# Up projection of a gated MLP: split weights in half units, spread over a column's seven products

## The chip, the cores and the metric

The kernel runs on one core of a Trainium2 chip. The metric is the device time of one execution in microseconds (us); in the profiled execution 1.81 us of it lie outside the span that the profiler records. TensorE is called PE in the rows, VectorE DVE, ScalarE ACT, GpSimd POOL and SyncE, which issues the DMAs, SP.

## The reference, cut to what matters

One encoder block on 16 meta and 1024 tokens with a model width of 1024. Its mixers run first; the change lies in what follows them: the output projection with the second norm, the up projection with a short convolution and a gate, and the first steps of the down projection. D_FF is 2816.

```python
h = h + merged @ w_out

f = dw_conv_centred(rms_norm(h, norm_ffn_w) @ w_ffn_up, w_ffn_conv, b_ffn_conv)
fg, fu = _split(f, (D_FF, D_FF))
return h + (jax.nn.silu(fg) * fu) @ w_ffn_down
```

## The kernel before, in words

Every float32 product is made of three: each operand is split into a high part (a cast on ScalarE) and a low part (the operand less its high part, on VectorE), and TensorE adds hi x hi, hi x lo and lo x hi. For weights that is `wsplit` (cast L1078, low part L1079) in the up stage and `wload` (load L132, L135, L136) elsewhere.

The **out-projection** runs in two rounds of tokens, r = 0 and 1. Each output tile d takes two column blocks, which VectorE evicts from PSUM with the residual added (L1052); ScalarE squares them and GpSimd adds the squares up (L1059). Behind round 0 comes its norm, in three steps (`scale`, `first`, `rest`) that are issued behind tiles d = 1, 2, 3 of round 1: a product with ones, a square root and reciprocals (L1017), eight multiplications on VectorE (L1022), sums on GpSimd (L1026, L1027, L1035) and the splits of seven operands b11, t2, t1, t3, b21, t4, b22 (L1008, L1009). Round 1's norm runs inside the first column of the up stage.

The **up stage** goes over 22 columns j. A column is one product of 2 x 2 blocks in a Strassen-Winograd scheme: seven block products of 12 matmuls each, in the two rounds (256 and 258 token columns), in the order b11, t2, t1, t3, b21, t4, b22, both rounds of a product together from column 1 on. Its weights a11, a12, a21, a22 come in two loads of 512 KB (L1090) into two raw buffers. Four sums on GpSimd (L1098 to L1101) make the combined blocks and are written over the raw ones. The splits of a column are three tiles of 1024 columns (each two blocks) and one of 512, in a ring of five tiles, and stand behind products b11/t2, t3, b21 and t4.

PSUM is evicted with the scheme's additions: ScalarE copies b11 and b21 (L1136, L1156), VectorE adds for t2 (L1141), t3 and t1 (L1151, L1152), t4 (L1160) and b22 (L1164). Then comes the convolution of the column before, over the two halves of f: a middle tap on GpSimd (L1174), two side taps on VectorE (L1175, L1176), Silu on ScalarE (L1178), the gate's product on GpSimd (L1181) and the store of `act` (L1182).

The **down stage** loads act tiles, splits them (L1236, L1237) and its own weights (`wload`), multiplies (PSUM tile psw) and adds (L1258).

Each engine runs its instructions in one fixed order, made when the kernel is built; a waiting instruction holds up what stands behind it. Tiles are reused in rings: a write waits for the last reader of the buffer's tile before.

## Time and profile before

| | |
|---|---|
| median of 3 runs | 2532.42 us (2527.24 to 2540.96) |
| profiled execution | 2529.71 us |
| its span | 2527.9 us |
| granted TensorE clock, mean | 0.977 |
| busy: PE / DVE / ACT / POOL | 94% / 51% / 31% / 34% of the span |
| up stage | about 1762 to 2255 us of the span |

The busy share is a mean over stages with different limits. The granted clock is in parts of full speed: 1.00 is 2.4 GHz, 0.50 is 1.2 GHz, and a value between them means that a stretch held both. An idle time in brackets names what ended it.

### The profile page before, as it was taken

The page shows a single profiled execution, that of the slowest core. Times are in us where ns is not written, and L with a number is a line of the kernel's source. Part 1 is how long each engine was busy: PE and PEld are TensorE (multiplying, and loading weights), DVE is VectorE, ACT ScalarE, POOL GpSimd, SP SyncE. Part 2 cuts the span into 40 slices and gives each one's busy share as a digit, 9 for nine tenths or more (in the row PEclk, how much of TensorE's full clock was granted, in tenths as well). Part 3 has the DMA queues.
Part 4 walks back from the last instruction along what each step waited for, and adds up shares of the span by engine and source line. Part 5 has one row for each costly group of instructions (what it writes and reads, how often), then busy time and mean ns, then how long its engine had stood idle before and what let it go on. Part 6 is the DMA issues. An engine that isn't in the chain of part 4 may idle for free. (4 is left out here: it accounts for less than half of the span.)

```text
span 2527.9 us, 38787 instructions
## 1 busy us (share of the span) xinstructions
PE 2387.7 (94%) x15836; PEld 2230.3 (88%) x15836; DVE 1290.1 (51%) x1822; ACT 771.7 (31%) x1320; POOL 853.9 (34%) x873
## 2 busy tenths in 40 slices
PE   7999999999899899989998999998899999989997
PEld 6999999988798788879887999997799999978887
DVE  6243344545635643663474442436766666665437
ACT  4312211333432532443234221223322222222204
POOL 2121222135514623641461122224355555540003
PEclk9999999999899999999998999999899999999999
DMA  4111112125723751572466552353122122245112
GB/s 146 50 48 41 51 49 61 54 87 158 167 55 126 164 104 63 175 157 45 139 169 168 175 151 90 98 156 113 60 81 76 68 75 76 76 148 194 67 49 68
DMA packets 132499, 259.09 MB, mean 102 GB/s; under 512 B 17441, under 2 KB 75297, under 8 KB 128225
## 3 DMA queue, kind: packets, MB, share of 16 engines
q1 hardware_dynamic: 132320, 256.62, 34.6%
q8 instruction: 124, 2.03, 0.4%
q14 instruction: 55, 0.44, 0.1%
HBM read 199.36 MB, written 57.20 MB: 101 GB/s over the span
## 5 line engine op out<-in xcount | busy, mean ns | idle before, releaser
L143 PE MATMUL psd<-uh,whi 128*128 128x342 f32 (+3 forms) x1376 | 462.5, 336 | 6.8 <-ACT gs L289 6.8
L144 PE MATMUL psd<-ul,whi 128*128 128x342 f32 (+3 forms) x1376 | 443.5, 322 | 0.0
L145 PE MATMUL psd<-uh,wlo 128*128 128x342 f32 (+3 forms) x1376 | 442.6, 322 | 0.0
L136 DVE TENSOR_TENSOR wlo<-wraw,whi 128x1024 fp32r<-128x1024 f32 (+1 forms) x144 | 190.5, 1323 | 217.1 <-ACT whi L135 216.8
L135 ACT CAST whi<-wraw 128x1024 fp32r<-128x1024 f32 (+1 forms) x144 | 149.3, 1039 | 482.7 <-PE psd L144 281.6
L143 PEld LDWEIGHTS psd<-uh,whi 128*128 128x128 f32 (+1 forms) x1376 | 261.1, 190 | 15.7 <-issue 7.2
L144 PEld LDWEIGHTS psd<-ul,whi 128*128 128x128 f32 (+1 forms) x1376 | 260.5, 189 | 7.1 <-issue 6.8
L145 PEld LDWEIGHTS psd<-uh,wlo 128*128 128x128 f32 (+1 forms) x1376 | 260.5, 189 | 0.1
L143 PE MATMUL psd<-whi,uh 128*128 128x256 f32 x768 | 232.6, 303 | 0.6 <-ACT uh L217 0.6
L145 PE MATMUL psd<-whi,ul 128*128 128x256 f32 x768 | 216.0, 281 | 3.3 <-POOL ul L219 2.7
L144 PE MATMUL psd<-wlo,uh 128*128 128x256 f32 x768 | 216.1, 281 | 0.0
L1079 DVE TENSOR_TENSOR wlo<-wraw,whi 128x1024 fp32r<-128x1024 f32 x88 | 112.6, 1284 | 113.7 <-ACT whi L1078 113.6
L143 PEld LDWEIGHTS psd<-whi,uh 128*128 128x128 f32 x768 | 145.3, 189 | 11.9 <-issue 9.1
L143 PE MATMUL psw<-ah,whi 128*128 128x512 f32 (+1 forms) x400 | 148.5, 373 | 5.9 <-ACT ah L1236 5.9
L144 PEld LDWEIGHTS psd<-wlo,uh 128*128 128x128 f32 x768 | 145.7, 190 | 5.8 <-issue 5.3
L144 PE MATMUL psw<-al,whi 128*128 128x512 f32 (+1 forms) x400 | 149.0, 373 | 1.0 <-DVE al L1237 1.0
L145 PEld LDWEIGHTS psd<-whi,ul 128*128 128x128 f32 x768 | 145.1, 189 | 4.1 <-POOL ul L219 3.1
L145 PE MATMUL psw<-ah,wlo 128*128 128x512 f32 (+1 forms) x400 | 146.4, 367 | 0.0
L1078 ACT CAST whi<-wraw 128x1024 fp32r<-128x1024 f32 x88 | 81.5, 940 | 201.4 <-POOL wraw L1101 100.3
L143 PE MATMUL psd<-krh,whi 128*128 128x342 f32 x384 | 123.6, 322 | 3.2 <-ACT krh L932 3.2
L144 PE MATMUL psd<-krl,whi 128*128 128x342 f32 x384 | 123.7, 322 | 0.3 <-DVE krl L933 0.3
L145 PE MATMUL psd<-krh,wlo 128*128 128x342 f32 x384 | 123.4, 322 | 0.0
(304 smaller groups left out, 6123.3 us busy)
## 6 DMA issues: line engine op xcount, KB each, us to landing
br<-row SPq DMA_DIRECT2D x32, 1024.0 KB
wraw<-in_w_up SPq DMA_DIRECT2D x44, 512.0 KB
gt<-gate SPq DMA_DIRECT2D x72, 171.0 KB
wraw<-in_w_xbc SPq DMA_DIRECT2D x24, 512.0 KB
act<-hb SPq DMA_DIRECT2D x22, 512.0 KB
ar<-act SPq DMA_DIRECT2D x22, 512.0 KB
wraw<-in_w_dn SPq DMA_DIRECT2D x19, 512.0 KB
gate<-gs SPq DMA_DIRECT2D x48, 171.0 KB
```

The costliest lines, as they stand in the source:

```text
L135: nc.scalar.copy(hi[:, :n], raw[:, :n])
L136: nc.vector.tensor_sub(lo[:, :n], raw[:, :n], hi[:, :n].bitcast(F32))
L143: nc.tensor.matmul(ps, ah, bh, start=(i == 0), stop=False)
L144: nc.tensor.matmul(ps, ah, bl, start=False, stop=False)
L145: nc.tensor.matmul(ps, al, bh, start=False, stop=(i == n - 1))
L1078: nc.scalar.copy(hi[:, :n], src)
L1079: nc.vector.tensor_sub(lo[:, :n], src, hi[:, :n].bitcast(F32))
```

## The change

Weights are split in units of one block (512 columns): seven casts and seven low parts a column, into a ring of ten half tiles. Each split stands behind one of the seven products: those of column j + 1 called s4 to s7 behind the first four products of column j, s1 to s3 of column j + 2 behind its last three. The loads of column j + 2 are issued at the start of column j, into four raw buffers: two of `wraw` for odd columns, two rows of hb for even ones. The first sum (now L1102) goes to a buffer of its own. The convolution is spread likewise: both middle taps behind the first product, the side taps of one half behind the second, Silu and the other side taps behind the third, the gate's product behind the fifth. The norm is cut into 17 small steps: two token blocks by themselves, multiplications in groups of four on 256 or 258 columns (L1023), issued three at a time. The first four act tiles are loaded ahead into the raw buffers (L1234), and high and low part of act share one tile. In the changed kernel the product is L1132, the load L1095, the sums L1102, L1103, L1104 and L1117, the evictions L1149, L1154, L1164, L1165, L1169, L1173 and L1177, the convolution L1187, L1192, L1193, L1196 and L1199.

```diff
-        def scale():
-            for b0, bn in RB[r]:
-                ps = pm.tile([P, 512], F32, name="psn", tag="psm")
-                a = acc[:, b0 - t0:b0 - t0 + bn]
-                nc.tensor.matmul(ps[:, :bn], ones, a, start=True, stop=True)
-                nc.scalar.activation(a, ps[:, :bn], AF.Sqrt, bias=eps, scale=1.0 / D)
-                nc.vector.reciprocal(a, a)
-        def first():
-            for d in range(KT):
-                hs = hb[:, d, t0:t0 + m]
-                nc.vector.scalar_tensor_tensor(hs, hs, V("norm_ffn", d), acc[:, :m], op0=ALU.mult, op1=ALU.mult)
-                if d == 3:
-                    put("b11", u[0][0])
-            put("b22", u[1][1])
-            nc.gpsimd.tensor_sub(t1, u[0][1], u[0][0])
-            nc.gpsimd.tensor_sub(t3, u[1][1], u[0][1])
-            nc.vector.tensor_sub(t2, u[1][1], t1)
-            put("t2", t2)
-        def rest():
-            put("t1", t1)
-            put("t3", t3)
-            put("b21", u[1][0])
-            nc.gpsimd.tensor_sub(t4, u[1][0], t2)
-            put("t4", t4)
-        return [scale, first, rest]
+        def scale(q):
+            b0, bn = RB[r][q]
+            ps = pm.tile([P, 512], F32, name="psn", tag="psm")
+            x = acc[:, b0 - t0:b0 - t0 + bn]
+            nc.tensor.matmul(ps[:, :bn], ones, x, start=True, stop=True)
+            nc.scalar.activation(x, ps[:, :bn], AF.Sqrt, bias=eps, scale=1.0 / D)
+            nc.vector.reciprocal(x, x)
+        def norm(d0, q):
+            b0, bn = RB[r][q]
+            for d in range(d0, d0 + 4):
+                hs = hb[:, d, b0:b0 + bn]
+                nc.vector.scalar_tensor_tensor(hs, hs, V("norm_ffn", d), acc[:, b0 - t0:b0 - t0 + bn], op0=ALU.mult, op1=ALU.mult)
+        steps = [lambda: scale(0), lambda: norm(0, 0), lambda: scale(1), lambda: norm(0, 1),
+                 lambda: put("b11", u[0][0]), lambda: nc.gpsimd.tensor_sub(t1, u[0][1], u[0][0]),
+                 lambda: norm(4, 0), lambda: put("b21", u[1][0]), lambda: norm(4, 1), lambda: put("t1", t1),
+                 lambda: put("b22", u[1][1]), lambda: nc.gpsimd.tensor_sub(t3, u[1][1], u[0][1]),
+                 lambda: nc.vector.tensor_sub(t2, u[1][1], t1), lambda: put("t2", t2),
+                 lambda: nc.gpsimd.tensor_sub(t4, u[1][0], t2), lambda: put("t3", t3), lambda: put("t4", t4)]
+        return steps
 
...
-            if d in (1, 2, 3) and pend is not None:
-                pend[d - 1]()
+            if d and pend is not None:
+                run([(0, x) for x in pend[:3]])
+                pend = pend[3:]
         pend = norm2_steps(r, acc)
...
+    halves = [[], []]
+    for i in range(5):
+        pool, nb = (wp, 3) if i < 3 else (wx, 2)
+        for x, hl in zip(("whi", "wlo"), halves):
+            tl = pool.tile([P, 1024], F32R, name=x, tag=x, bufs=nb)
+            hl += [tl[:, :512], tl[:, 512:]]
     nwt = [0]
 
-    def wsplit(src, n):
-        pool = wp if nwt[0] % 5 < 3 else wx
+    def wsplit(src):
+        hi, lo = halves[0][nwt[0] % 10], halves[1][nwt[0] % 10]
         nwt[0] += 1
-        hi = pool.tile([P, 1024], F32R, name="whi", tag="whi", bufs=3 if pool is wp else 2)
-        lo = pool.tile([P, 1024], F32R, name="wlo", tag="wlo", bufs=3 if pool is wp else 2)
-        nc.scalar.copy(hi[:, :n], src)
-        nc.vector.tensor_sub(lo[:, :n], src, hi[:, :n].bitcast(F32))
+        nc.scalar.copy(hi, src)
+        nc.vector.tensor_sub(lo, src, hi.bitcast(F32))
         return hi, lo
 
-    def weights(j):
-        w = {}
-        def load():
-            w["r"] = r = []
+    class Weights:
+        def __init__(self, j):
+            self.j, self.w = j, {}
+        def load(self):
+            if self.j < 2 or self.j % 2:
+                r = [wp.tile([P, 1024], F32, name="wraw", tag="wraw", bufs=2) for _ in range(2)]
+            else:
+                r = [hb[:, q, :1024] for q in (2, 7)]
             for half in range(2):
-                raw = wp.tile([P, 1024], F32, name="wraw", tag="wraw", bufs=2)
-                nc.sync.dma_start(out=raw, in_=t["w_up"][half * NF + j])
-                r.append(raw)
-            w["a1"] = wsplit(r[0], 1024)
-        def sums():
-            r = w["r"]
-            a11, a12, a21, a22 = r[0][:, :512], r[0][:, 512:], r[1][:, :512], r[1][:, 512:]
-            w["a2"] = wsplit(a22, 512)
-            nc.gpsimd.tensor_tensor(a22, a21, a22, op=ALU.add)
+                nc.sync.dma_start(out=r[half], in_=t["w_up"][half * NF + self.j])
+            self.a = [r[0][:, :512], r[0][:, 512:], r[1][:, :512], r[1][:, 512:]]
+        def s1(self):
+            a11, a12, a21, a22 = self.a
+            self.w["a11"] = wsplit(a11)
+            self.x = sg.tile([P, 516], F32, name="ws1", tag="ka", bufs=3)[:, :512]
+            nc.gpsimd.tensor_tensor(self.x, a21, a22, op=ALU.add)
             nc.gpsimd.tensor_sub(a21, a11, a21)
-            nc.gpsimd.tensor_sub(a11, a22, a11)
-            nc.gpsimd.tensor_sub(a12, a12, a11)
-        def s24():
-            w["s24"] = wsplit(w["r"][0], 1024)
-        def s31():
-            w["s31"] = wsplit(w["r"][1], 1024)
-        return w, [load, sums, s24, s31]
+            nc.gpsimd.tensor_sub(a11, self.x, a11)
+        def s2(self):
+            self.w["s2"] = wsplit(self.a[0])
+        def s3(self):
+            self.w["s1"] = wsplit(self.x)
+        def s4(self):
+            self.w["s3"] = wsplit(self.a[2])
+        def s5(self):
+            self.w["a12"] = wsplit(self.a[1])
+            nc.gpsimd.tensor_sub(self.a[1], self.a[1], self.a[0])
+        def s6(self):
+            self.w["a22"] = wsplit(self.a[3])
+        def s7(self):
+            self.w["s4"] = wsplit(self.a[1])
 
-        key, half = {"b11": ("a1", 0), "b21": ("a1", 1), "t4": ("a2", 0), "t2": ("s24", 0), "b22": ("s24", 1),
-                     "t3": ("s31", 0), "t1": ("s31", 1)}[o]
-        hi, lo = w[key]
+        hi, lo = w[{"b11": "a11", "t2": "s2", "t1": "s1", "t3": "s3", "b21": "a12", "t4": "a22", "b22": "s4"}[o]]
...
-        def one(half):
+        def mid(half):
             fi = half * NF + j
             raw = f[half]
             nc.gpsimd.memset(raw[:, NB:NB + 1], 0.0)
             nc.gpsimd.tensor_scalar(o[half], raw[:, 2:2 + SEQ], V("fconv_w", 3 * fi + 1), V("fconv_b", fi), op0=ALU.mult, op1=ALU.add)
+        def sides(half):
+            fi = half * NF + j
+            raw = f[half]
             nc.vector.scalar_tensor_tensor(o[half], raw[:, 1:1 + SEQ], V("fconv_w", 3 * fi), o[half], op0=ALU.mult, op1=ALU.add)
             nc.vector.scalar_tensor_tensor(o[half], raw[:, 3:3 + SEQ], V("fconv_w", 3 * fi + 2), o[half], op0=ALU.mult, op1=ALU.add)
-            if half == 0:
-                nc.scalar.activation(o[0], o[0], AF.Silu)
+        def gate():
+            nc.scalar.activation(o[0], o[0], AF.Silu)
 
...
-        return [lambda: one(0), lambda: one(1), fin]
-    w, prep = weights(0)
-    for f_ in prep:
-        f_()
-    conv = [lambda: None] * 3
+        return [lambda: (mid(0), mid(1)), lambda: sides(0), lambda: (gate(), sides(1)), lambda: None, fin,
+                lambda: None, lambda: None]
+    none = [lambda: None] * 7
+    act_raw = {}
+    W = [Weights(j) for j in range(NF)]
+    W[0].load()
+    for x in ("s1", "s2", "s3", "s4", "s5", "s6", "s7"):
+        getattr(W[0], x)()
+    W[1].load()
+    for x in ("s1", "s2", "s3"):
+        getattr(W[1], x)()
+    conv = none
     for j in range(NF):
-        nxt, prep = weights(j + 1) if j + 1 < NF else (None, [lambda: None] * 4)
         f = [hb[:, q, :] for q in ((0, 1) if j % 2 == 0 else (5, 6))]
-        ra, rb_ = up_round(w, f, 0), up_round(w, f, 1)
+        ra, rb_ = up_round(W[j].w, f, 0), up_round(W[j].w, f, 1)
+        n1 = W[j + 1] if j + 1 < NF else None
+        n2 = W[j + 2] if j + 2 < NF else None
+        prep = [n1 and n1.s4, n1 and n1.s5, n1 and n1.s6, n1 and n1.s7, n2 and n2.s1, n2 and n2.s2, n2 and n2.s3]
         if j == 0:
-            ra[0]()
-            ra[1]()
-            pend[0]()
-            ra[2]()
-            ra[3]()
-            pend[1]()
-            for p_ in ra[4:]:
-                p_()
-            pend[2]()
-            rb_[0]()
-            rb_[1]()
-        else:
-            for p_ in (ra[0], rb_[0], ra[1], rb_[1]):
-                p_()
-        prep[0]()
-        conv[0]()
-        for q in (2, 3):
+            at = {0: 3, 1: 3, 2: 2, 3: 3, 4: 2, 5: 2, 6: 2}
+            for q in range(7):
+                ra[q]()
+                run([(0, x) for x in pend[:at[q]]])
+                pend = pend[at[q]:]
+        if n2:
+            n2.load()
+        elif j == NF - 1:
+            for q in range(2):
+                act_raw[q] = wp.tile([P, 1024], F32, name="wraw", tag="wraw", bufs=2)
+            for q in range(2):
+                act_raw[2 + q] = hb[:, (2, 7)[q], 0:SEQ]
+            for q in range(4):
+                nc.sync.dma_start(out=act_raw[q], in_=act_d[q])
+        for q in range(7):
             if j:
                 ra[q]()
             rb_[q]()
-        prep[1]()
-        conv[1]()
-        for q, g in ((4, prep[2]), (5, prep[3]), (6, conv[2])):
-            if j:
-                ra[q]()
-            rb_[q]()
-            g()
-        w = nxt
+            if prep[q]:
+                prep[q]()
+            conv[q]()
         conv = conv_steps(j, f)
-    ROW = (2, 7, 0, 1, 5, 6, 3, 4)
+    ROW = (0, 1, 2, 7, 5, 6, 3, 4)
...
     def act_load(j):
-        raw = fp.tile([P, SEQ], F32, name="ar", tag="ar", bufs=4)
-        nc.sync.dma_start(out=raw, in_=act_d[j])
-        acth[j] = fp.tile([P, SEQ], F32R, name="ah", tag="ah", bufs=11)
-        actl[j] = fp.tile([P, SEQ], F32R, name="al", tag="al", bufs=11)
+        a = fp.tile([P, 2, SEQ], F32R, name="ahl", tag="ahl", bufs=11)
+        raw = act_raw.pop(j, None)
+        if raw is None:
+            raw = fp.tile([P, SEQ], F32, name="ar", tag="ar", bufs=4)
+            nc.sync.dma_start(out=raw, in_=act_d[j])
+        acth[j], actl[j] = a[:, 0, :], a[:, 1, :]
         nc.scalar.copy(acth[j], raw)
         nc.vector.tensor_sub(actl[j], raw, acth[j].bitcast(F32))
```

The next two fences show **VectorE** in a steady column, between the evictions of t3 and t1 of one column and of t2 of the next, before and then changed. wlo is the low part of weights, psu a PSUM tile; hb holds f, the convolution's halves and, in the changed kernel, raw weights too; ws1 is the first sum.

```order
L1079 TENSOR_TENSOR wlo_19411<-wraw_19343,whi_19410 128x512
L1160 TENSOR_TENSOR hb_12744<-psu_19380,hb_12744 128x256
L1160 TENSOR_TENSOR hb_12744<-psu_19395,hb_12744 128x258
L1079 TENSOR_TENSOR wlo_19479<-wraw_19343,whi_19478 128x1024
L1079 TENSOR_TENSOR wlo_19449<-wraw_19341,whi_19448 128x1024
L1164 TENSOR_TENSOR hb_12744<-psu_19354,hb_12744 128x256
L1164 TENSOR_TENSOR hb_12744<-psu_19367,hb_12744 128x256
L1175 SCALAR_TENSOR_TENSOR hb_12744<-hb_12744,vec_72 128x1024 x2
```

```order
L1079 TENSOR_TENSOR wlo_16553<-wraw_18630,whi_16552 128x512
L1173 TENSOR_TENSOR hb_12744<-psu_18732,hb_12744 128x256
L1173 TENSOR_TENSOR hb_12744<-psu_18747,hb_12744 128x258
L1079 TENSOR_TENSOR wlo_16555<-wraw_18630,whi_16554 128x512
L1177 TENSOR_TENSOR hb_12744<-psu_18701,hb_12744 128x256
L1192 SCALAR_TENSOR_TENSOR hb_12744<-hb_12744,vec_72 128x1024
L1177 TENSOR_TENSOR hb_12744<-psu_18714,hb_12744 128x256
L1079 TENSOR_TENSOR wlo_16555<-ws1_18792,whi_16554 128x512
L1193 SCALAR_TENSOR_TENSOR hb_12744<-hb_12744,vec_72 128x1024
L1192 SCALAR_TENSOR_TENSOR hb_12744<-hb_12744,vec_72 128x1024
L1079 TENSOR_TENSOR wlo_16547<-wraw_18631,whi_16546 128x512
L1193 SCALAR_TENSOR_TENSOR hb_12744<-hb_12744,vec_72 128x1024
```

The splits moved from two pairs of long ones to half units between the evictions and the side taps; all four side taps now stand ahead of t2's evictions.

**GpSimd** in the same place, before and then changed, from one gate's product to the next:

```order
L1181 TENSOR_TENSOR hb_12744<-hb_12744 128x1024
L1098 TENSOR_TENSOR wraw_18218<-wraw_18218 128x512
L1099 TENSOR_TENSOR wraw_18218<-wraw_18216,wraw_18218 128x512
L1100 TENSOR_TENSOR wraw_18216<-wraw_18218,wraw_18216 128x512
L1101 TENSOR_TENSOR wraw_18216<-wraw_18216 128x512
L1173 MEMSET hb_12744 128x1
L1174 TENSOR_SCALAR hb_12744<-hb_12744,vec_72 128x1024 x2
```

```order
L1199 TENSOR_TENSOR hb_12744<-hb_12744 128x1024
L1117 TENSOR_TENSOR wraw_17738<-wraw_17738 128x512
L1104 TENSOR_TENSOR hb_12744<-ws1_18122,hb_12744 128x512
L1102 TENSOR_TENSOR ws1_18346<-wraw_18185 128x512
L1103 TENSOR_TENSOR wraw_18185<-wraw_18184,wraw_18185 128x512
L1186 MEMSET hb_12744 128x1
L1187 TENSOR_SCALAR hb_12744<-hb_12744,vec_72 128x1024 x2
```

The four sums now belong to three successive columns: L1117 to the first, L1104 to the second, and L1102 and L1103, which read a new load, to the third. In every other column L1102 stands ahead of L1104.

**VectorE at the end of the up stage**, before and then changed, from the eviction of the last b22 on; L136 is the low part of a down weight, L1237 and L1259 that of an act tile:

```order
L1164 TENSOR_TENSOR hb_12744<-psu_21384,hb_12744 128x256
L1176 SCALAR_TENSOR_TENSOR hb_12744<-hb_12744,vec_72 128x1024
L1175 SCALAR_TENSOR_TENSOR hb_12744<-hb_12744,vec_72 128x1024
L136 TENSOR_TENSOR wlo_21699<-wraw_21696,whi_21698 128x1024
L1176 SCALAR_TENSOR_TENSOR hb_12744<-hb_12744,vec_72 128x1024
L1237 TENSOR_TENSOR al_21520<-ar_21517,ah_21519 128x1024
```

```order
L1177 TENSOR_TENSOR hb_12744<-psu_21375,hb_12744 128x256
L1193 SCALAR_TENSOR_TENSOR hb_12744<-hb_12744,vec_72 128x1024
L1259 TENSOR_TENSOR ahl_21507<-wraw_21294,ahl_21507 128x1024
L1259 TENSOR_TENSOR ahl_21510<-wraw_21295,ahl_21510 128x1024
L1259 TENSOR_TENSOR ahl_21513<-hb_12744,ahl_21513 128x1024
L1259 TENSOR_TENSOR ahl_21516<-hb_12744,ahl_21516 128x1024
L1192 SCALAR_TENSOR_TENSOR hb_12744<-hb_12744,vec_72 128x1024
L1259 TENSOR_TENSOR ahl_21544<-ar_21545,ahl_21544 128x1024
L1193 SCALAR_TENSOR_TENSOR hb_12744<-hb_12744,vec_72 128x1024
L136 TENSOR_TENSOR wlo_21541<-wraw_21538,whi_21540 128x1024
```

The first low part of a down weight moved from ahead of the act splits, where it was the third of its kind, to behind five of them; its load goes into a buffer (wraw) that the first act split reads.

## Rows read from the trace of the kernel before

**Rows 1.** Stretches: length, busy PE, PEld, DVE, ACT, POOL, PE clock, DMA share, GB/s.

```profile
1740.00:1760.00 20.00, 14.38 (x105) 14.14 (x105) 11.83 (x15) 6.51 (x8) 7.61 (x4) 0.91 0.41 119
1760.00:1780.00 20.00, 15.16 (x98) 14.07 (x97) 10.81 (x14) 5.04 (x8) 6.88 (x5) 0.83 0.19 67
1780.00:1800.00 20.00, 13.38 (x86) 12.76 (x86) 16.99 (x16) 8.04 (x10) 7.99 (x5) 0.83 0.10 27
```

**Rows 2.** TensorE's waits from 1740 to 2270 us: total us, times, longest.

```profile
PE psu L1119 <- ACT whi L1078: 15.4, 10, 5.7
PE psu L1119 <- DVE wlo L1079: 10.2, 15, 0.8
```

**Rows 3.** Timeline, TensorE: start of columns 2 and 3, last matmul of column 21.

```profile
1829.05 0.28 PE L1119 MATMUL psu<-b11h,wlo 128*128 128x256 f32 x1
...
1848.81 0.28 PE L1119 MATMUL psu<-b11h,whi 128*128 128x256 f32 x1
...
2254.35 0.28 PE L1119 MATMUL psu<-b22h,wlo 128*128 128x258 f32 x1
```

**Rows 4.** Timeline, TensorE: the long stalls, idle us before in brackets.

```profile
1744.08 0.48 PE L143 MATMUL psd<-mh,whi 128*128 128x256 f32 x1 [4.05 <-DVE hb L1052]
...
1767.09 0.39 PE L1119 MATMUL psu<-t2h,whi 128*128 128x256 f32 x1 [3.56 <-ACT whi L1078]
...
1789.77 0.58 PE L1119 MATMUL psu<-t3h,whi 128*128 128x258 f32 x1 [5.11 <-ACT t3h L1008]
...
1812.97 0.58 PE L1119 MATMUL psu<-t2h,whi 128*128 128x256 f32 x1 [5.65 <-ACT whi L1078]
...
2260.56 0.79 PE L143 MATMUL psw<-ah,whi 128*128 128x512 f32 x1 [5.93 <-ACT ah L1236]
```

**Rows 5.** GpSimd's sums by line and shape, 1830 to 2233 us: busy us, mean ns.

```profile
L1100 POOL TENSOR_TENSOR wraw<-wraw 128x512 f32<-128x512 f32 x19 | 24.6, 1293 | 1.5
```

**Rows 6.** Timeline, VectorE and GpSimd: two meetings of the two engines.

```profile
1862.67 2.41 POOL L1181 TENSOR_TENSOR hb<-hb 128x1024 f32<-128x1024 f32 x1 [3.68 <-DVE hb L1152]
...
1863.33 2.29 DVE L1079 TENSOR_TENSOR wlo<-wraw,whi 128x512 fp32r<-128x512 f32 x1
...
1893.58 1.19 POOL L1174 TENSOR_SCALAR hb<-hb,vec 128x1024 f32<-128x1024 f32 x1
...
1896.47 1.28 DVE L1175 SCALAR_TENSOR_TENSOR hb<-hb,vec 128x1024 f32<-128x1024 f32 x1
...
1896.71 2.10 POOL L1174 TENSOR_SCALAR hb<-hb,vec 128x1024 f32<-128x1024 f32 x1 [1.94 <-issue]
```

**Rows 7.** Timeline, ScalarE and VectorE: half cast, Silu, half split, eviction.

```profile
1885.07 0.62 ACT L1078 CAST whi<-wraw 128x512 fp32r<-128x512 f32 x1 [0.64 <-ACT hb L1156]
...
1904.03 1.06 ACT L1178 ACTIVATE hb<-hb 128x1024 f32<-128x1024 f32 x1 [7.02 <-DVE hb L1176]
...
1802.58 0.69 DVE L1079 TENSOR_TENSOR wlo<-wraw,whi 128x512 fp32r<-128x512 f32 x1
...
1902.38 0.42 DVE L1141 TENSOR_TENSOR hb<-psu,hb 128x256 f32<-128x256 f32 x1
```

**Rows 8.** Timeline, SyncE and ScalarE: two weight loads, the casts behind them.

```profile
1873.52 0.33 SPq L1090 DMA_DIRECT2D wraw<-in_w_up  x1
...
1878.08 1.06 ACT L1078 CAST whi<-wraw 128x1024 fp32r<-128x1024 f32 x1 [4.63 <-DMA wraw<-in_w_up]
...
1892.46 0.33 SPq L1090 DMA_DIRECT2D wraw<-in_w_up  x1
...
1895.68 1.05 ACT L1078 CAST whi<-wraw 128x1024 fp32r<-128x1024 f32 x1 [0.79 <-DMA wraw<-in_w_up]
```

**Rows 9.** Timeline, VectorE: one piece of the normalization.

```profile
1778.47 0.74 DVE L1022 SCALAR_TENSOR_TENSOR hb<-hb,vec,acc 128x514 f32<-128x514 f32 x1
```

**Rows 10.** Timeline, SyncE and VectorE: first w_dn load, last column's convolution.

```profile
2237.33 0.33 SPq L132 DMA_DIRECT2D wraw<-in_w_dn  x1
...
2256.42 1.27 DVE L1176 SCALAR_TENSOR_TENSOR hb<-hb,vec 128x1024 f32<-128x1024 f32 x1
```

More of the change, by code (lines that the diff above doesn't have):

```diff
@@ L1116, in product @@
         for k in range(4):
-            c = slice(half * 512 + k * P, half * 512 + (k + 1) * P)
+            c = slice(k * P, (k + 1) * P)
             for i, (a, b) in enumerate(((hi, xh), (hi, xl), (lo, xh))):
```

## Prediction

> **What bounds the kernel now.** I read the windows first, then TensorE's waits, then the starts of the columns, then what VectorE and GpSimd do beside them. TensorE sets the end nearly everywhere, so the change is worth what it takes out of TensorE's waits in the up stage and what it adds to them.
>
> The stage has two parts. At its start TensorE idles a quarter of the time: of the 60 us from 1740 to 1800 it is busy 14.38, 15.16 and 13.38, and the granted clock is 0.91 and then 0.83 [rows 1]. The long stalls there are on an eviction of the out-projection (4.05), on the first t2 weights (3.56), on t3 of the second round (5.11) and on column 1's t2 weights (5.65) [rows 4]. From column 2 on the stalls are short but come in nearly every column: 15 waits on wlo and most of the 10 on whi [rows 2]. Column 2 alone runs without one: it begins at 1829.05, column 3 at 1848.81, so a stall-free column takes 19.76 us; columns 2 to 21 end at 2254.63 (the last matmul's start plus its 0.28), 425.6 us or 21.28 us a column [rows 3]. That leaves 1.5 us a column, about 30 us in all, for the steady part.
>
> Why t2 is late: its weights are a sum of sums (L1098 to L1101, 1.29 each [rows 5]) that can start only after the split of a22, which waits for one of five whole ring tiles.
>
> **VectorE and GpSimd in turns.** The rows that decide this case are meetings of the two. A half split takes 0.69 alone [rows 7], but the one that starts at 1863.33, while GpSimd's product L1181 runs to 1865.08, takes 2.29: it ends 0.54 after GpSimd does. The middle tap L1174 takes 1.19 alone and 2.10 when a side tap of VectorE (1896.47, 1.28) is under way [rows 6]. So VectorE's operations on two SBUF tiles and GpSimd's go one after the other, whichever came first. The eviction from PSUM (0.42 [rows 7]) is not of this kind. The Trainium skill's page "SBUF — State Buffer", section "Who interferes with whom", has the same rule: a VectorE instruction with two SBUF inputs and a GpSimd instruction that reads SBUF take a shared port pair in turns, each for the whole instruction. The trace agrees, 2.29 against 0.69.
>
> After the change a column holds seven half splits (7 x 0.69), four side taps (4 x 1.28), four sums (4 x 1.29), two middle taps (2 x 1.19) and one product (2.41): 4.8 + 5.1 + 5.2 + 2.4 + 2.4 = 19.9 us of work in turns. TensorE needs 19.76. If the two engines did not exclude each other, a column would be TensorE's 19.76; since they do, the new order has no slack from the start, and any wait inside it lengthens the column.
>
> **Term 1, columns 2 to 21.** TensorE's waits on whi and wlo go: splits run some nine products ahead in a ring of ten halves. What is late next is the evictions, because VectorE runs in order. TensorE's t4 needs the eviction of t3 of its own column. Between t3's first half and t4's first half lie three half products (3 x 19.76/14 = 4.2 us), so VectorE may lag 3.8 us (4.2 less an eviction) before TensorE waits at t4. Lag comes from a loop through three queues that closes once a column. The weights of column j+2 go into the buffers of column j; SyncE can issue the load only after VectorE's last split of column j (s7), and GpSimd's next sum waits for the landing, with the middle taps queued behind it. VectorE's side taps wait for the middle taps, and behind them stand the evictions. Step by step, from the end of s7, where the order is L1117, L1104, L1102:
>
> load to use 3.2 (1892.46 to 1895.68; the other pair 4.56) [rows 8]; sums L1102 and L1103, 2 x 1.37 (1.29 and a start gap); memset and middle tap 1.3; side tap 1.28; eviction, half split and second side tap 2.1 (0.42 + 0.69 + 1.28, less about 0.1 each by which I let an end overlap the next start, here and below); middle tap of the other half, blocked by those, 1.1; side tap 1.28, half split 0.6, side tap 1.2; Silu 1.06; product 2.4, which blocks the split behind it; two half splits 1.3; L1117 1.29; cast 0.62; s7 0.69. Together 22.2.
>
> In every other column L1102 stands ahead of L1104 and its load was issued a split earlier, so one sum falls into the shadow of the landing: 20.8. The mean is 21.5. This is a chain put together from single rows, and hand-offs may lengthen it; it is nearly as long as the present 21.28. Eighteen columns (2 to 19) at 21.5, less the one lag of 3.8, and two last columns at 19.76, since they load nothing: 387.0 - 3.8 + 39.5 = 422.7, against 425.6. **Term 1 is -3 us.** Its bounds: -30 if the loop hides (20 x 1.52), +22 if every landing takes 4.56 (18 x 1.36 = 24.5 more).
>
> **Term 2, columns 0 and 1.** Column 1's first three splits now stand before column 0's products, so the 5.65 goes. The 3.56 stays: the first load still waits for the last split of the out-projection. The 5.11 was t3 waiting for the whole of the norm; with small steps t3 comes earlier, but b11 of the second round waits for the same norm, with sums and splits of column 1 in between. I take half, 2.5. The clock of 0.83 over 40 us costs 0.17 x 40 = 6.8 [rows 1]; with half the idle time I give back a quarter, 1.7. **Term 2 is -10** (5.65 + 2.5 + 1.7); from -2, if b11 takes over the 5.11 and the 5.65 both, to -20.
>
> **Term 3, out-projection.** The norm of round 0 goes in 16 pieces of 256 in place of 8 of 512, with evictions in between. A piece of 514 columns takes 0.74 [rows 9]; one of 256 is not shown; between half of it, 0.37, and 0.74 I take 0.45, since a 256-wide eviction takes 0.42 [rows 7]: 16 x 0.45 - 8 x 0.74 = +1.3 us of VectorE, which hides in its idle time (8.2 of 20 us from 1740 [rows 1]). The eviction that TensorE waited 4.05 for no longer stands behind eight such pieces. Of 4.05 I take 3, since GpSimd's sums still meet the pieces. **Term 3 is -3**, from -4 to +5.
>
> **Term 4, into the down stage.** Before, the first down weights are loaded at 2237.33, 17 us before the last product ends [rows 10], and TensorE waits 5.93 only for the split of act [rows 4]. Now act 0 to 3 are loaded early and lie in the raw buffers, so the first down load waits for the first act split (L1259), which stands behind both side taps of the last column. The second of those ends at 2257.69 [rows 10]; a split of 1024 is about two halves, 1.3; load 3.2, cast 1.05 [rows 8]: 2263.2, against TensorE's 2260.56. **Term 4 is +2**, from 0 (the split lands earlier than its place) to +4.
>
> **Sum:** -3 - 10 - 3 + 2 = -14 on the profiled execution's 2529.7, which gives 2516. The median of the runs shown, 2532.4, lies 2.7 higher, so I say 2517. About 0.5%, 12.7 us, is what a measurement of this kernel can tell from no change; the forecast lies just beyond it.
>
> **Rivals.**
> - *TensorE-bound columns.* If the landing hides, say because TensorE's stalls at the start let the loads run ahead, the loop is 19.0 and 17.6 us, under 19.76, and term 1 is -30: 2529.7 - 30 - 11 = 2489. For it: a load takes only 3.2 us. Against: 19.9 us of work in turns leave no room. Chance 0.28.
> - *The start gives nothing.* b11 of round 1 stalls where t3 did and the norm's pieces queue behind sums: terms 2 and 3 are -2 and 0, and the time is 2527. For it: VectorE is busy 17 of 20 us at 1780 to 1800 [rows 1], and the change puts column 1's work there. Chance 0.17.
> - *Slower: blocked sums.* Each of three GpSimd sums starts while a half split runs, as the 2.10 tap did, at 0.69 each: the loop is 23.6, term 1 is 18 x 23.6 + 35.7 - 425.6 = +35, and the time is 2554. It decides from a loop of 22.3 on, where 18 x 22.3 + 35.7 - 425.6 = +11 eats terms 2 to 4. For it: splits are now spread over the whole column, so more of them meet a sum. Against: blocked time is partly time that the chain already counts. Chance 0.15.
> - *The forecast*, with terms 2 and 3 as taken and columns of 21.1 to 21.9: 2510 to 2526. Chance 0.40.
>
> **How the numbers follow.** The range reaches from just under the TensorE-bound case to between no change and the blocked one, 2486 to 2542, and leaves out some 1 in 10 on either side. Faster by over 0.5% is the TensorE-bound case and half of the forecast, 0.48; within 0.5% the rest of the forecast, the start that gives nothing and a little of the slow case, 0.37; slower 0.15.
>
> **What would show it.** Right: no waits on whi or wlo after column 2; TensorE's waits there are on VectorE evictions (L1164) at t4; GpSimd idle before L1102 on a DMA, about 3 us a column; columns near 21.5, and 19.8 in the last two; no stall over 5 us in column 1; the first down product some 2 us later after the last up product. Wrong: columns of 19.8 throughout, with GpSimd never waiting for a load, or columns over 22.3 with sums well above 1.29. The weakest step is the landing inside the loop: if the loads are issued a split earlier than I read, the whole gain of term 1 is there.

## The result and the profile after

The changed kernel takes 2547.63 us (median of 11 runs, 2541.49 to 2553.32), the kernel before 2533.17 (11 runs beside it, 2527.24 to 2540.96). The ratio is 1.0054, with a 95% interval of 1.004 to 1.0069: slower by about 14 us, where 16 us less had been forecast.

The profiled execution took 2553.32 us, its span is 2551.3. In it the out-projection begins 10.5 us later than in the execution of before (at 1668.69, where the trace of before has its first row at 1658.15); that lies ahead of everything that the change touches, so the stages are compared by their own lengths, each from one profiled execution. The timeline of TensorE shows their bounds: the first product of the out-projection, of the up stage, of columns 2, 3, 4 and 20, the last one of the up stage, and the first of the down stage. A row gives start, duration, engine, line and shapes. In the trace of before the out-projection and the up stage begin at:

```profile
1658.15 0.28 PE L143 MATMUL psd<-mh,whi 128*128 128x256 f32 x1
...
1761.94 0.28 PE L1119 MATMUL psu<-b11h,whi 128*128 128x256 f32 x1
```

and in that of the changed kernel the bounds are:

```profile
1668.69 0.28 PE L143 MATMUL psd<-mh,whi 128*128 128x256 f32 x1
...
1771.41 0.28 PE L1132 MATMUL psu<-b11h,whi 128*128 128x256 f32 x1
...
1842.22 0.28 PE L1132 MATMUL psu<-b11h,whi 128*128 128x256 f32 x1
...
1862.12 0.28 PE L1132 MATMUL psu<-b11h,whi 128*128 128x256 f32 x1
...
1883.29 0.28 PE L1132 MATMUL psu<-b11h,whi 128*128 128x256 f32 x1
...
2234.69 0.28 PE L1132 MATMUL psu<-b11h,whi 128*128 128x256 f32 x1
...
2274.66 0.28 PE L1132 MATMUL psu<-b22h,wlo 128*128 128x258 f32 x1
...
2284.43 0.79 PE L143 MATMUL psw<-ahl,whi 128*128 128x512 f32 x1 [9.48 <-ACT whi L135]
```

| us | before | after | forecast of the difference | measured |
|---|---|---|---|---|
| out-projection (term 3) | 103.8 | 102.7 | -3 | -1.1 |
| columns 0 and 1 (term 2) | 67.1 | 70.8 | -10 | +3.7 |
| columns 2 to 21 (term 1) | 425.6 | 432.7 | -3 | +7.1 |
| from the last up product to the first down product (term 4) | 5.9 | 9.5 | +2 | +3.6 |

The four differences sum to +13.3; the down stage behind them is 0.5 us shorter than before (266.9 for 267.4). TensorE's waits from 1740 to 2290 us (total, times, longest; six rows of the view) answer to [rows 2]:

```profile
PE psu L1132 <- DVE hb L1164: 26.2, 16, 3.7
PE psw L143 <- ACT whi L135: 9.5, 1, 9.5
PE psd L143 <- DVE hb L1046: 6.7, 2, 5.4
PE psu L1132 <- ACT b11h L1008: 3.2, 1, 3.2
PE psn L1015 <- POOL acc L1053: 3.0, 1, 3.0
PE psu L1132 <- ACT t3h L1008: 2.2, 1, 2.2
```

No wait of any length on whi or wlo is left from column 2 on, as the change intends. In their place stand 14 of the 16 waits on the eviction of t3 (L1164), all at t4: 21.5 us in columns 2 to 21, where whi and wlo cost 16.4 before. The other two fall in columns 0 and 1 (0.95 and 3.69). The windows of columns 0 and 1 and of columns 2 to 21, the kernel before first, give behind the bounds the length and TensorE's busy time; the rest of the length is idle. The granted clock is the third figure from the end:

```profile
1761.94:1829.05 67.11, 49.85 (x345) 47.73 (x344) 46.24 (x49) 21.05 (x29) 30.05 (x24) 0.87 0.18 60
1829.05:2254.63 425.58, 409.16 (x3360) 403.52 (x3358) 271.36 (x361) 118.10 (x181) 225.80 (x176) 1.00 0.22 79
...
1771.41:1842.22 70.81, 53.19 (x342) 50.89 (x341) 62.65 (x73) 25.13 (x41) 41.33 (x29) 0.81 0.21 71
1842.22:2274.94 432.72, 411.20 (x3362) 408.09 (x3360) 296.16 (x412) 124.43 (x235) 226.92 (x171) 0.98 0.22 75
```

In columns 0 and 1 the idle time is nearly the same (17.3 and 17.6 us) and the busy time grew by 3.3, at a lower clock; in columns 2 to 21 the idle time grew by 5.1 and the busy time by 2.0. One column shows the loop. The rows are of GpSimd, VectorE, SyncE and TensorE, in order of time:

```profile
2069.98 2.40 POOL L1199 TENSOR_TENSOR hb<-hb 128x1024 f32<-128x1024 f32 x1 [4.26 <-ACT hb L1196]
...
2075.36 0.69 DVE L1079 TENSOR_TENSOR wlo<-wraw,whi 128x512 fp32r<-128x512 f32 x1 [0.25 <-ACT whi L1078]
...
2076.08 0.33 SPq L1095 DMA_DIRECT2D wraw<-in_w_up  x1
...
2079.34 1.49 POOL L1102 TENSOR_TENSOR ws<-wraw 128x512 f32<-128x512 f32 x1 [1.06 <-DMA wraw<-in_w_up]
...
2080.91 1.29 POOL L1103 TENSOR_TENSOR wraw<-wraw 128x512 f32<-128x512 f32 x1
...
2082.23 1.20 POOL L1187 TENSOR_SCALAR hb<-hb,vec 128x1024 f32<-128x1024 f32 x1
...
2083.46 1.28 DVE L1192 SCALAR_TENSOR_TENSOR hb<-hb,vec 128x1024 f32<-128x1024 f32 x1 [3.47 <-POOL hb L1187]
...
2085.24 2.62 POOL L1187 TENSOR_SCALAR hb<-hb,vec 128x1024 f32<-128x1024 f32 x1 [1.81 <-issue]
...
2092.16 2.39 POOL L1199 TENSOR_TENSOR hb<-hb 128x1024 f32<-128x1024 f32 x1 [4.26 <-ACT hb L1196]
...
2096.09 0.39 PE L1132 MATMUL psu<-t4h,whi 128*128 128x256 f32 x1 [1.84 <-DVE hb L1164]
```

The split s7 (2075.36) ends, and SyncE issues the load at 2076.08. GpSimd's first sum L1102 sits idle until it lands and starts at 2079.34, the next follows, and only then the middle tap (2082.23). VectorE waits 3.47 us for it before its side tap. The second middle tap takes 2.62 instead of 1.20, blocked by VectorE. From one gate's product (2069.98) to the next (2092.16) pass 22.18 us, and TensorE then waits 1.84 for the eviction behind it. In GpSimd's timeline the nine cycles of this kind took 22.05 to 22.59 us. Of the eight where L1102 stands ahead of L1104, six took 21.20 to 21.38 and two, in which L1103 also waited for its load, 21.74 and 22.27. GpSimd's idle time just before L1102 was 1.1 to 1.7 us in the first kind and 2.4 to 2.6 in the second. From column 4 to column 20 a column takes 21.96 us on the mean (1883.29 to 2234.69, 16 columns); the two last, which load nothing, take 20.12 and 20.13.

At the start the stalls moved. These are the timeline's rows of TensorE for four of them, with the idle time before each in brackets, and the windows that answer to [rows 1]:

```profile
1779.52 0.80 PE L1015 MATMUL psn<-acc,cst 128*128 128x258 f32 x1 [3.02 <-POOL acc L1053]
...
1791.22 0.38 PE L1132 MATMUL psu<-b11h,whi 128*128 128x258 f32 x1 [3.20 <-ACT b11h L1008]
...
1804.42 0.39 PE L1132 MATMUL psu<-t3h,whi 128*128 128x258 f32 x1 [2.18 <-ACT t3h L1008]
...
1833.93 0.58 PE L1132 MATMUL psu<-t4h,whi 128*128 128x256 f32 x1 [3.69 <-DVE hb L1164]
```

```profile
1740.00:1760.00 20.00, 13.00 (x83) 12.32 (x82) 20.00 (x19) 8.30 (x9) 9.65 (x5) 0.74 0.36 105
1760.00:1780.00 20.00, 14.84 (x117) 14.23 (x116) 12.03 (x15) 6.31 (x12) 10.18 (x7) 0.95 0.35 98
1780.00:1800.00 20.00, 14.25 (x71) 13.18 (x71) 18.72 (x28) 6.73 (x11) 6.52 (x4) 0.67 0.10 36
```

The 5.65 on column 1's t2 is gone, t3 of round 1 waits 2.18 instead of 5.11, and the first t2 weights are waited for 1.9 instead of 3.56 [rows 4]. But the product with ones waits 3.02 (1.0 before) for GpSimd's sum of squares (L1053), which stands behind the first up-weight sums; b11 of round 1 waits 3.20; and column 1's t4 already waits 3.69 for an eviction. All waits of columns 0 and 1 sum to 17.6 us, 17.3 before, and the granted clock over the two columns is 0.81 where it was 0.87.

At the end, the first act split, the load that waited for it and the cast of that load:

```profile
2276.62 1.22 DVE L1259 TENSOR_TENSOR ahl<-wraw,ahl 128x1024 fp32r<-128x1024 f32 x1
...
2277.86 0.33 SPq L132 DMA_DIRECT2D wraw<-in_w_dn  x1
...
2283.33 1.04 ACT L135 CAST whi<-wraw 128x1024 fp32r<-128x1024 f32 x1 [3.83 <-DMA wraw<-in_w_dn]
```

The load is issued as the first act split ends (2277.86), as forecast, but its cast waits until 2283.33, 5.5 us and not 3.2. Act and h loads are in flight at the same time; no run shows what the landing takes without them.

### The profile page after: what moved, and what is told of

It is laid out like the page before. It is cut to its first block, busy times and chain, and to the rows that moved or that the text cites. A ratio compares the mean times of both kernels' runs of the same rounds, so it can differ in the third digit from the quotient of the medians.

```text
span 2551.3 us, 39054 instructions
## 1 busy us (share of the span) xinstructions
PE 2401.9 (94%) x15836; PEld 2246.6 (88%) x15836; DVE 1340.5 (53%) x1904; ACT 780.7 (31%) x1386; POOL 865.6 (34%) x873
## 5 line engine op out<-in xcount | busy, mean ns | idle before, releaser
L136 DVE TENSOR_TENSOR wlo<-wraw,whi 128x1024 fp32r<-128x1024 f32 (+1 forms) x144 | 185.8, 1290 | 222.2 <-ACT whi L135 222.2
L143 PEld LDWEIGHTS psd<-whi,uh 128*128 128x128 f32 x768 | 148.2, 193 | 11.5 <-issue 8.9
L143 PE MATMUL psw<-ahl,whi 128*128 128x512 f32 (+1 forms) x400 | 148.0, 370 | 9.5 <-ACT whi L135 9.5
L145 PE MATMUL psw<-ahl,wlo 128*128 128x512 f32 (+1 forms) x400 | 148.7, 373 | 0.3 <-DVE wlo L136 0.3
L144 PE MATMUL psw<-ahl,whi 128*128 128x512 f32 (+1 forms) x400 | 147.7, 369 | 0.0
L1280 DVE TENSOR_TENSOR hb<-psw,hb 128x512 f32<-128x512 f32 x80 | 55.2, 690 | 106.7 <-PE psw L145 106.5
L690 POOL TENSOR_SCALAR cacc<-craw,vec 128x1040 f32<-128x1040 f32 x24 | 42.4, 1766 | 191.1 <-ACT craw L687 191.1
```

What stands on the lines that cost most here:

```text
L136: nc.vector.tensor_sub(lo[:, :n], raw[:, :n], hi[:, :n].bitcast(F32))
L143: nc.tensor.matmul(ps, ah, bh, start=(i == 0), stop=False)
L144: nc.tensor.matmul(ps, ah, bl, start=False, stop=False)
L145: nc.tensor.matmul(ps, al, bh, start=False, stop=(i == n - 1))
L690: nc.gpsimd.tensor_scalar(acc, raw[:, 1:L + 1], V("conv_w", 3 * f + 1), V("conv_b", f), op0=ALU.mult, op1=ALU.add)
L1280: nc.vector.tensor_tensor(hs, ps, hs, op=ALU.add)
```

## The experiments

All are variants of the changed kernel, except where said. Ratios are to the kernel before, run beside them; its own median was 2530.3 to 2536.9 us from group to group, so ratios are compared and not times. The last three columns are from one profiled execution each: "columns" is the mean over columns 4 to 19, "wait" the idle time of TensorE before the first down product.

| run | ratio (95%) | columns 0, 1 | columns | wait |
|---|---|---|---|---|
| before | 1 | 67.1 | 21.32 | 5.9 |
| changed kernel | 1.0054 (1.004 to 1.0069) | 70.8 | 21.96 | 9.5 |
| middle tap on ScalarE | 0.9914 (0.9893 to 0.9935) | 67.6 | 19.98 | 9.4 |
| no loads of up weights | 0.9927 (0.9912 to 0.9942) | 74.6 | 19.98 | 9.0 |
| load behind the middle taps | 0.9984 (0.9971 to 0.9998) | 68.0 | 20.93 | 9.0 |
| eight halves, splits later | 1.0005 (0.9994 to 1.0017) | 69.1 | 21.37 | 9.1 |
| the same, six raw buffers | 1.0018 (1.0005 to 1.0031) | 72.0 | 21.34 | 9.3 |
| old steps of the norm | 1.0047 (1.003 to 1.0064) | 68.0 | 21.95 | 9.4 |
| no early act loads (one execution) | 2541.5 us | 72.9 | 21.99 | 3.2 |
| middle tap on ScalarE, no early act loads | 0.9885 (0.9859 to 0.9911) | 68.4 | 19.98 | 3.1 |
| the same, column 1's splits later | 0.9905 (0.9885 to 0.9925) | 71.1 | 19.98 | 3.1 |
| kernel before, middle tap on ScalarE | 0.9951 (0.9932 to 0.997) | 64.9 | 20.78 | 5.3 |

**The middle tap on ScalarE.**

```diff
-            nc.gpsimd.tensor_scalar(o[half], raw[:, 2:2 + SEQ], V("fconv_w", 3 * fi + 1), V("fconv_b", fi), op0=ALU.mult, op1=ALU.add)
+            nc.scalar.activation(o[half], raw[:, 2:2 + SEQ], AF.Identity, bias=V("fconv_b", fi), scale=V("fconv_w", 3 * fi + 1))
```

> The changed kernel with the convolution's middle tap on ScalarE in place of GpSimd (two of 1.2 us a column leave the work in turns, and the side taps no longer stand behind the sums that wait for a load). By theory A and by theory B alike the loop opens: VectorE is no longer held at the first side tap, work in turns falls from 19.9 to 17.5 us, and columns are TensorE's 19.8 to 20.2: 2547.6 less 17 x 1.8 to 2.1, about 2512 to 2518. A rival that the columns are long because VectorE itself has too much in its queue would leave them at 21 or more, 2533 or more.

2507.19 us, columns of 19.98: the columns came as expected, the time is a little below the expected 2512 to 2518, and the ratio is below that of both kernels. From 1860 to 2230 us TensorE has no wait that the view lists. Its timeline has the starts of columns 4 and 20, GpSimd's the sum that waits for a load:

```profile
1867.74 0.28 PE L1132 MATMUL psu<-b11h,whi 128*128 128x256 f32 x1
...
2187.47 0.28 PE L1132 MATMUL psu<-b11h,whi 128*128 128x256 f32 x1
...
2062.58 1.28 POOL L1102 TENSOR_TENSOR ws<-hb 128x512 f32<-128x512 f32 x1 [2.33 <-DMA hb<-in_w_up]
```

The landing is still there (2.33 us idle before the sum), but nothing of VectorE's stands behind it any more. By itself this run can't tell the landing from the turns, since it takes away both.

**No loads of up weights.**

```diff
+            if self.j > 2:
+                p = W[self.j - 2]
+                r = [p.r[0], p.r[1]]
+            else:
+                for half in range(2):
+                    nc.sync.dma_start(out=r[half], in_=t["w_up"][half * NF + self.j])
+            self.r = r
-            for half in range(2):
-                nc.sync.dma_start(out=r[half], in_=t["w_up"][half * NF + self.j])
```

> The changed kernel without the loads of up weights from column 3 on: the sums and splits go on with what lies in the raw buffers (so the up product's weights are not the reference's), every other instruction stays. Theory A, the landing closes the loop: nothing waits for a landing, the loop of 21.96 us loses 3.5 to 4 us, and columns are TensorE's 19.8 to 20.3: 2542 to 2548 less 17 x 1.7 to 2.1, about 2507 to 2518. Theory B, turns alone: GpSimd's wait for the landing only fills time in which VectorE uses the shared turn, so columns stay at 21.3 or more, 2533 or more. Between them (20.5 to 21.2): the landing is a part and turns the rest.

2518.36 us, at the end of the expected 2507 to 2518, columns of 19.98. All work in turns is still there, and the columns are TensorE's: in this order the turns alone don't lengthen a column. Rows of GpSimd (middle taps L1192 and first sum L1107 here) and the starts of columns 4 and 20:

```profile
2055.07 1.20 POOL L1192 TENSOR_SCALAR hb<-hb,vec 128x1024 f32<-128x1024 f32 x1
...
2058.84 2.62 POOL L1192 TENSOR_SCALAR hb<-hb,vec 128x1024 f32<-128x1024 f32 x1 [2.56 <-ACT whi L1078]
...
2061.43 1.28 POOL L1107 TENSOR_TENSOR ws<-wraw 128x512 f32<-128x512 f32 x1
...
1877.27 0.28 PE L1137 MATMUL psu<-b11h,whi 128*128 128x256 f32 x1
...
2197.00 0.28 PE L1137 MATMUL psu<-b11h,whi 128*128 128x256 f32 x1
```

The second middle tap is blocked for 2.62 us as before, and it costs nothing. Without the load to wait for, the order of GpSimd also came out otherwise, with both middle taps ahead of the sum; the next run separates the two.

**The load behind the middle taps.**

```diff
+                if half and gate is not None:
+                    nc.gpsimd.tensor_scalar(r[1][:, 0:1], gate, 1.0, 0.0, op0=ALU.mult, op1=ALU.add)
                 nc.sync.dma_start(out=r[half], in_=t["w_up"][half * NF + self.j])
...
-        if n2:
+        if n2 and j == 0:
             n2.load()
...
-            if prep[q]:
+            if prep[q] and q:
                 prep[q]()
             conv[q]()
+            if q == 0:
+                if n2 and j:
+                    n2.load(hb[:, 3, 0:1])
+                if prep[q]:
+                    prep[q]()
```

> The changed kernel with one order changed: the second raw load of column j+2 is issued only after the middle taps of column j-1's convolution (a one-element operation of GpSimd on the buffer makes it wait), so that GpSimd's sum that waits for this load stands behind the middle taps, not ahead of them. All loads stay, and the landing comes later than before. Theory A (the landing costs because the middle taps, and with them VectorE's side taps and evictions, stand behind it): columns 19.9 to 20.7, 20 to 35 us less than the changed kernel, ratio to the kernel before 0.988 to 0.996. Rival (it is the transfer itself, its traffic or its buffers, that costs, and the run without loads was fast because it moved nothing): columns stay at 21.4 or more.

2527.55 us: 20.93 a column, outside the expected 19.9 to 20.7, as is the ratio (0.9984 for 0.988 to 0.996), and below the rival's 21.4. The variant also puts the split s4 behind the middle taps, but in the traces VectorE and ScalarE run in the order of the changed kernel and only GpSimd's order differs. The loads are all there and land later, and the columns are 1.03 us shorter by that order. What is left of the landing is seen at GpSimd's first sum (L1104 here) and the gate's product behind it (L1201):

```profile
2053.68 1.30 POOL L1104 TENSOR_TENSOR ws<-hb 128x512 f32<-128x512 f32 x1 [3.41 <-DMA hb<-in_w_up]
...
2056.84 2.86 POOL L1201 TENSOR_TENSOR hb<-hb 128x1024 f32<-128x1024 f32 x1
```

The sum still waits 3.41, now ahead of the gate's product. From 1900 to 2200 us GpSimd is idle 49.1 us before this sum, always for a load, against 26.2 before L1102 in the changed kernel: a longer wait, at a place where it costs less. In the run without loads the three engines run in the order of this run, but for the one-element operation, so the loads that are waited for make the other 0.95 us a column (20.93 to 19.98).

**Ring and raw buffers.** Two first tries, a ring of eight halves and the same with six raw buffers, are no test: the program writes ten halves ahead, so that in a ring of eight a half is written over before the product of its column has read it; the up products use other weights and wait for later splits.

> The changed kernel with a ring of eight half tiles in place of ten and nothing else. It is the control for the six raw buffers. By theory A (the landing in the loop) and by theory B (turns alone) the ring is no limit: columns 21.6 to 22.3 us, 2540 to 2555. By theory C (the splits that run too far ahead take VectorE and GpSimd from the convolution) columns fall below 21.2 and the time to 2535 or less.

> The changed kernel with six raw weight buffers in place of four (three sets in turn), and, to make room, a ring of eight half tiles in place of ten. Theory A, the loop through the landing: the load of column j+2 is issued a column earlier, so the first sum no longer waits for it, the loop loses the 3.5 to 4 us of landing, and columns fall from 21.96 to 19.9 to 20.6 us: 2547.6 less 17 x 1.4 to 2.0, about 2513 to 2524. Theory B, turns alone: VectorE's and GpSimd's 19.9 us of work in turns with Silu and the casts between them set the column whatever the load does: columns stay at 21.5 or more, 2540 or more. Theory C, the ring is what matters: then the kernel with eight halves alone moves as much as this one.

They took 2543.12 (ratio 1.0053) and 2541.69 us (1.0051), with columns of 21.09 and 21.07, and nothing is drawn from them. The next two keep seven splits ahead, which a ring of eight holds; the second adds a pair of raw buffers.

```diff
-        prep = [n1 and n1.s4, n1 and n1.s5, n1 and n1.s6, n1 and n1.s7, n2 and n2.s1, n2 and n2.s2, n2 and n2.s3]
+        prep = [n1 and n1.s1, n1 and n1.s2, n1 and n1.s3, n1 and n1.s4, n1 and n1.s5, n1 and n1.s6, n1 and n1.s7]
...
-        hi, lo = halves[0][nwt[0] % 10], halves[1][nwt[0] % 10]
+        hi, lo = halves[0][nwt[0] % 8], halves[1][nwt[0] % 8]
```

> The changed kernel with a ring of eight half tiles and, so that this ring holds, column j+1's seven splits all written behind column j's products (seven products ahead instead of ten; none of column 1's splits ahead of column 0). Theory A (landing in the loop): the load still follows the last split and the sums still wait for it, so columns stay at 21 to 22 us. Theory C (splits too far ahead crowd the side taps): columns fall below 20.8. At the start, three half splits fewer stand among the second norm's pieces: b11's wait of 3.2 + 1.6 us should fall to 2 to 3 in all, but column 1's first weights come later, so columns 0 and 1 together change by less than 4 us.

> The same as the kernel with eight halves and the later splits, with six raw buffers instead of four, so that the load of column j+2 does not wait for column j's last split. Theory A: the landing is out of the loop, columns 19.8 to 20.6, and 10 to 25 us less than with four. Theory B (turns alone): no difference to four buffers beyond 4 us.

2537.87 and 2540.92 us, columns of 21.37 and 21.34. Theory A's 21 to 22 held with four buffers and its 19.8 to 20.6 missed with six, where theory B had no difference. With six buffers GpSimd's first sum waits for up loads only 1.5 us in all from 1900 to 2200, and with four only 5.5: in this order the landing is nearly out either way, and the columns stay. The rows point at another loop, through the gate's product (L1203), the split behind it (L1080) and the eviction of t3 (L1168) in GpSimd's and VectorE's timelines:

```profile
2064.25 2.40 POOL L1203 TENSOR_TENSOR hb<-hb 128x1024 f32<-128x1024 f32 x1 [2.26 <-ACT hb L1200]
...
2064.71 2.49 DVE L1080 TENSOR_TENSOR wlo<-ws,whi 128x512 fp32r<-128x512 f32 x1 [0.97 <-ACT whi L1079]
...
2067.72 0.41 DVE L1168 TENSOR_TENSOR hb<-psu,hb 128x256 f32<-128x256 f32 x1
```

The split starts 0.46 us after the product, ends 0.55 after it, and the eviction that TensorE's t4 needs stands behind it. So the landing is not the only thing that can lengthen a column: with the taps and sums in another order it takes 21.3 almost without it, by these rows through the turns. No run takes this one meeting away; with the splits as late and the middle taps on ScalarE (next to last in the table) the columns are 19.98.

**Old steps of the norm.** The norm function and its calls are those of the kernel before.

> The changed kernel with the norm in its old three steps of whole 512 columns. Columns from 2 on stay at 21.9. If the small steps did their part, the start gets worse by 3 to 8 us (out-projection's stalls 6.7 back to 7.6 or more, b11 and t3 of round 1 later): 2550 to 2556. If the small steps are what costs at the start (VectorE's evictions and pieces blocked by GpSimd's sums), it gets better by 2 to 6 us, 2541 to 2545.

2546.87 us, neither case: the out-projection takes 103.8 us (102.7 with small steps) and columns 0 and 1 take 68.0 (70.8). b11 and t3 of round 1 wait 4.0 each. The small steps move the waits and give nothing that this measurement can tell from no change (1.0047 and 1.0054).

**No early act loads.**

```diff
-        elif j == NF - 1:
-            for q in range(2):
-                act_raw[q] = wp.tile([P, 1024], F32, name="wraw", tag="wraw", bufs=2)
...
-            for q in range(4):
-                nc.sync.dma_start(out=act_raw[q], in_=act_d[q])
```

> The changed kernel without the early loads of the first four act tiles, so that the raw buffers are free for the first down weights, as before. Theory: the first down product waits 9.5 us in the changed kernel because its weights' load stands behind the first act split; without the early loads the wait is near the 5.9 us of before (5.5 to 6.5), now for an act split, and the time is 3 to 4 us shorter. Rival: the wait is set by the last column's convolution on VectorE; then it stays at 8 us or more.

TensorE's waits from 2200 to 2290 us on the down stage's operands:

```profile
PE psw L144 <- DVE ahl L1252: 3.3, 1, 3.3
PE psw L143 <- ACT ahl L1251: 3.2, 1, 3.2
```

6.5 us in two waits, 9.5 + 0.3 with the early loads, 5.9 + 1.0 before. The wait before the first down product is 3.2, below the expected 5.5 to 6.5, and a second one of 3.3 follows. In these two traces the early loads cost 3.3 us by taking the raw buffers from the first down weights.

**Together.** Middle tap on ScalarE and no early act loads; then also none of column 1's splits ahead of column 0; and the kernel before with the middle tap on ScalarE alone.

> The changed kernel with the middle tap on ScalarE and without the early act loads. If the two costs add: columns 20.0, the first down product 3 us earlier than with the middle tap alone (9.4 us of waiting down to 6 to 7), ratio to the kernel before 0.989 to 0.992.

> As the kernel with the middle tap on ScalarE and no early act loads, with none of column 1's splits written ahead of column 0's products. At the start b11's waits (3.2 + 1.6) fall by 2 to 3 us and column 1's first weights come 1 to 3 us late: columns 0 and 1 within 3 us of the other, and no measurable difference.

> The kernel before with the middle tap on ScalarE and nothing else. There t2's weights are late because a22's split waits for a whole ring tile and the sums follow it; the middle taps stand behind the sums and take turns with the splits. Theory (ring and chain of sums): columns fall only from 21.3 to 20.9 to 21.2, 2 to 8 us less, so the middle tap on ScalarE pays only together with the change. Rival (turns limit the kernel before as well): columns 20.3 or less, 18 us or more.

The first takes 2503.04 us against 2530.33 beside it, the lowest ratio of all; it is not told apart from the middle tap alone, whose interval overlaps its own. The second, 2507.86, is not told apart from it either. The kernel before gains 0.5% (0.3 to 0.7) from the tap alone, 11.5 us where 2 to 8 were expected, and keeps the waits of t2, as TensorE's list from 1820 to 2250 us shows:

```profile
PE psu L1119 <- DVE wlo L1079: 8.5, 15, 0.8
...
PE psu L1119 <- ACT whi L1078: 0.8, 4, 0.2
```

## Why the prediction was wrong, point by point

**Term 2, columns 0 and 1, is the step that failed**: 13.7 of the 27 us between the sum of -14 and the measured +13.3. It counted the 5.65 and half of the 5.11 as gained, and the rows show the first gone and the second down by 2.9. What it did not ask is what is late next there, beyond b11. The waits moved to the product with ones, to b11 and to t4, and came to 17.6 us in place of 17.3: idle time was cut into other pieces and not reduced. The clock, which the term took to come back by 1.7 us, fell from 0.87 to 0.81, and TensorE was busy 53.2 us where it had been 49.9; these 3.3 us are most of the +3.7. The rival that the start gives nothing (0.17) had the ground that showed, VectorE busy 18.72 of 20 us, b11 waiting and GpSimd's queue holding the sum of squares; but its time of 2527 is 20 us short too. Columns 0 and 1 take 67.6 us or more in every variant of the changed kernel, so no run comes near the forecast 57. Why the waits moved is read from rows; no run takes the new ones away. Which order would shorten the start stays open: the old norm gave 68.0 and later splits for column 1 69.1, but the run without early act loads, with the same code in these columns as the changed kernel, took 72.9 against its 70.8, so that differences of 2 or 3 us between single executions tell nothing.

**Term 1 was right in its mechanism, and its sum came out 10.1 us too low.** The waits on whi and wlo went, the evictions at t4 became the wait, GpSimd waited for the landing (1.1 to 2.6 us a column, where about 3 was named as a sign), the two last columns ran at 20.1. The runs with the later load and without loads show the cause: of the 1.98 us by which a column exceeds TensorE's 19.98, the landing's place ahead of the middle taps makes 1.03, and the wait for loads that is left makes 0.95. Sizes were off. The loop of 22.2 was measured at 22.05 to 22.59. That of the other columns, taken at 20.8, took 21.20 to 21.38 in six of eight: a sum did fall into the shadow of the landing and the middle tap starts 1.2 us earlier in the cycle, but a split blocks it and it takes 1.60 in place of 1.20. And most of the lag of 3.8 us that was to be had once was spent before column 2: t4 of column 1 already waited 3.69, and only columns 2 and 3 (19.90 and 21.17) ran ahead of the loop. So columns 2 to 19 took 392.5 us (1842.22 to 2234.69) in place of 383.2. The case that the work in turns (19.9 us by the rows) leaves a column no room did not hold as an argument against TensorE-bound columns: without loads they run at 19.98 with that work in them. In these runs a column took longer when something else waited inside it: the landing, or, in the runs with later splits and by their rows alone, a split behind the gate's product. The Trainium skill's page "SBUF — State Buffer", section "Who interferes with whom", gives the turns themselves, and the rows agree (2.49 and 2.62 for operations of 0.69 and 1.20). How much they cost depended here on the order.

**Term 3** was -1.1 for -3: an eviction still waited, 5.4 us at the longest, now behind three low parts of the norm on VectorE (1745.32 to 1750.91), one of which took 3.33 in place of 1.21, blocked by GpSimd's sum L1028.

**Term 4** had the right cause and +3.6 for +2: the landing took 5.5 us among other loads where 3.2 was taken from the steady state. The run without early act loads gives the 3.3 us back.

Two slips in the working carry little: term 4's own figures give +2.6 (2263.2 less 2260.56) where +2 was entered, and 2516 with 2.7 more is 2518.7, not 2517.

Of the rivals, the one of TensorE-bound columns is what the kernel does without the loads, or with the taps on ScalarE. Columns 2 to 21 take 399.9 us then, 25.7 less than before, where 30 was said: a column without a stall takes 19.98 on the mean, not 19.76. The changed kernel does not get there. Blocked sums, the rival on the slow side, was not the way it became slower: GpSimd's middle tap and L1117 were stretched (2.62 and 1.60 to 1.66 us), but they are in the run without loads too (2.62 and 1.67), at 19.98 a column.

## What to carry to other kernels

An engine that waits for a load should have nothing behind that wait in its queue that another engine needs: moving one wait behind two short operations was worth 0.7%, with all transfers kept. When stalls are taken out of a stage whose other engines are nearly full, work out what is late next for each of them, since the same idle time can come back under another name, as it did in columns 0 and 1. And where two engines take turns, try giving one of their operations to a third: the middle tap on ScalarE, which was busy 28 us in 100, gained 0.5% in the kernel before, where the whole rearrangement by itself lost 0.5%.

## What the runs showed of the hardware

ScalarE does the middle tap (scale and bias by partition, 128x1024) in 1.24 to 1.25 us, all 44 times in the run that moves it there, with VectorE and GpSimd at work beside it; GpSimd takes 1.20 alone and 2.62 blocked. A blocked operation can wait for two operations of the other engine in a row: GpSimd's 1.20 tap that started at 2085.24 took 2.62, to 2087.86, behind a split (2084.99 to 2085.67) and a side tap (2085.59 to 2086.87) that followed each other without a gap. In the steady columns of the changed kernel the granted clock fell to its lower level, 1.2 GHz, five times, each time with a stall of 1.78 to 2.39 us; a stall of 1.84 us (2096.09) had no fall with it, and the kernel before has one fall, behind stalls of 0.92 and 0.76 us (near 2109). The four runs whose steady columns have no stall have none. A column with such a fall took 23.5 to 24.0 us and the next one 19.9 to 20.7, so that most of the loss came out of the waiting time behind it.
